# Instance normalisation over 65536 rows: sharing a tile's reductions between ScalarE and VectorE

## The chip, the core and the metric

The kernel runs on one core of one Trainium2 chip. Times are device microseconds of one execution; "span" is the time from the first to the last instruction in a profiled execution, some 2 us less than the execution's own time. ScalarE is ACT in the profile, VectorE is DVE, and SP is the engine whose queue issues every transfer here (SPq and DVEq in the profile are the instruction queues of SP and VectorE). A transfer has landed when its semaphore has its full count; its time to landing runs from its issue to then, so it includes waiting behind earlier transfers.

## The reference

```python
def reference(x, eps):            # x: 256 x 256 x 4096 float32, standard normal
    mean = np.mean(x, axis=2, keepdims=True)
    var = np.var(x, axis=2, keepdims=True)
    return ((x - mean) / np.sqrt(var + eps)).astype(np.float32)
```

So 65536 rows of 4096 numbers, each normalised by itself: 1.07 GB in, as much out, and only a few operations on each number.

## The kernel before

A tile is 128 partitions x 4 rows x 4096 numbers, 8.389 MB, and there are 128 tiles. Three buffers `X[0..2]` hold a tile each; a tile is normalised in place and stored from the same buffer. The first and the last tile are done in two halves of two rows. Semaphores order everything by hand.

SP's loop issues the store of tile t as soon as it is normalised, and right after it the load of tile t+2 into the buffer of tile t-1, whose store was issued a period earlier:

```python
def store(s, t):
    take(S, done[s], K)                      # all K=4 rows normalised
    S.dma_start(out=rows_of(out_t, t), in_=X[s][:, :, :]).then_inc(stored[s], 16)

def load(s, t, wait=True):
    if wait:
        take(S, stored[s], 16)               # the buffer's last store has landed
    S.dma_start(out=X[s][:, :, :], in_=rows_of(x_t, t)).then_inc(loaded[s], 16)
...
with S.Fori(0, rounds) as i:
    for t in range(L0, L0 + BUFS):
        store(t % BUFS, ...)
        load((t + 2) % BUFS, ...)
```

VectorE takes the means of all four rows, one after the other; ScalarE follows a row behind with the sum of squares around the mean (its output goes to a scrap tile in PSUM, and only the accumulated sum is used). Then VectorE normalises rows 0, 1 and 3, ScalarE row 2:

```python
def vector_tile(s, r0=0, k=K, ld=None, dn=None):
    ...
    if ld:
        take(V, ld, 16)
    for r in range(r0, r0 + k):
        ...
        mine(V.tensor_reduce(out=part[s][:, r, :], in_=row, axis=AX.X, op=ALU.add))
        V.wait_ge(own_v, own)
        mine(V.tensor_reduce(out=nsum[s][:, c], in_=part[s][:, r, :], axis=AX.X, op=ALU.add, negate=True))
        V.wait_ge(own_v, own)
        V.tensor_scalar_mul(out=nmean[s][:, c], in0=nsum[s][:, c], scalar1=1.0 / d).then_inc(means, 1)
    last = r0 + k - 1
    for i, c in enumerate((slice(r0, last), slice(last, last + 1))):
        ...                                  # wait for std; rstd and nbias
        for r in range(r0, last - 1) if i == 0 else (last,):
            c = slice(r, r + 1)
            V.tensor_scalar(out=x[:, r, :], in0=x[:, r, :], scalar1=rstd[s][:, c], scalar2=nbias[s][:, c],
                            op0=ALU.mult, op1=ALU.add).then_inc(dn, 1)

def scalar_tile(s, r0=0, k=K, ld=None, dn=None):
    ...
    for r in range(r0, r0 + k):
        ...                                  # wait for the row's mean
        A.activation(out=junk, in_=x[:, r, :], func=AF.Square, bias=nmean[s][:, c], scale=1.0,
                     accum_out=ss[s][:, c]).then_inc(own_a, 1)
    ...                                      # Sqrt; wait for `scaled`
    A.activation(out=x[:, last - 1, :], in_=x[:, last - 1, :], func=AF.Identity,
                 bias=nbias[s][:, c], scale=rstd[s][:, c]).then_inc(dn, 1)
```

## Time and profile before

| | before |
|---|---|
| median of 3 executions | 4965.49 us (4963.85 to 4969.12) |
| span of the profiled execution | 4960.3 us |
| VectorE busy | 3390.1 us (68%) |
| ScalarE busy | 2505.6 us (51%) |
| bytes moved | 2147.52 MB, mean 433 GB/s |

The costliest groups of instructions of the kernel before, from its page: line, engine, operation, what it writes and reads, sizes, count, then the busy time in all and the mean of one in ns, then the engine's idle time before them and what ended most of it.

```profile
L89 DVE TENSOR_REDUCE part<-x 128x64 f32<-128x4096 f32 x512 | 2258.6, 4411 | 1452.4 <-DMA x<-in_x_dram 1452.4
L132 ACT ACTIVATE junk<-x,nmean 128x4096 f32<-128x4096 f32 x512 | 1883.0, 3678 | 2417.0 <-DVE nmean L93 2417.0
L110 DVE TENSOR_SCALAR x<-x,rstd,nbias 128x4096 f32<-128x4096 f32 x382 | 910.2, 2411 | 37.6 <-DVE nbias L102 16.4
L140 ACT ACTIVATE x<-x,nbias,rstd 128x4096 f32<-128x4096 f32 x130 | 492.2, 3786 | 0.0
```

The first line is the dearest work of the kernel, a mean at 4.41 us, and the engine that does it is idle for 1452 us, all of it waiting for loads. ScalarE waits 2417 us for means. These two columns invite the change: ScalarE is idle for want of means, so let it make one.

### The profile page before, as it was taken

How to read it: one execution, taken by the hardware profiler on the slowest of the kernel's cores; microseconds unless marked ns; L12 is line 12 of the kernel's file. 1: busy time of each engine (PE TensorE's matmuls, PEld its weight loads, DVE VectorE, ACT ScalarE, POOL GpSimd, SP SyncE). 2: the span in 40 equal slices, each digit the busy share in tenths (PEclk: the TensorE clock that was granted, in tenths of full speed). 3: DMA queues.
4: the chain of work that ended last, by engine and by line, in shares of the span. 5: the costliest groups of instructions: out<-in, count | busy, mean ns of one | idle time of the engine just before them, and what ended most of it. 6: DMA issues, size and time to landing. Idle time of an engine off the chain costs nothing.

```text
span 4960.3 us, 6348 instructions
## 1 busy us (share of the span) xinstructions
DVE 3390.1 (68%) x2439; ACT 2505.6 (51%) x1416; POOL 0.2 (0%) x4
## 2 busy tenths in 40 slices
DVE  6766666776677766777667776677666776677766
ACT  5555544555445544555445554455544555455545
POOL 0000000000000000000000000000000000000000
DMA  9999999999999999999999999999999999999999
GB/s 423 431 435 430 431 434 433 433 436 433 433 436 432 434 436 432 435 435 433 437 432 434 436 432 434 436 432 433 437 432 434 435 433 435 435 432 438 432 433 406
DMA packets 37299, 2147.52 MB, mean 433 GB/s; under 512 B 4144, under 2 KB 4144, under 8 KB 4144
## 3 DMA queue, kind: packets, MB, share of 16 engines
q1 hardware_dynamic: 37296, 2147.50, 100.0%
q14 instruction: 3, 0.02, 0.0%
HBM read 1073.74 MB, written 1073.74 MB: 433 GB/s over the span
## 4 chain that ended last, share of the span: by engine, by line
DMA 71%; DVE 19%; ACT 7%; another core or an unknown queue 1%; issue 1%; SPq 0%; ACTq 0%; DVEq 0%
DMA x<-in_x_dram 40%; DMA out_dram<-x 31%; DVE part L89 17%; ACT junk L132 3%; ACT x L140 3%; DVE nsum L91 1%; DVE x L110 1%; DVE nmean L93 1%; ACTq L182 0%; ACT std L137 0%; DVE nbias L102 0%; SPq L159 0%; SPq L154 0%; DVE rstd L100 0%
## 5 line engine op out<-in xcount | busy, mean ns | idle before, releaser
L89 DVE TENSOR_REDUCE part<-x 128x64 f32<-128x4096 f32 x512 | 2258.6, 4411 | 1452.4 <-DMA x<-in_x_dram 1452.4
L132 ACT ACTIVATE junk<-x,nmean 128x4096 f32<-128x4096 f32 x512 | 1883.0, 3678 | 2417.0 <-DVE nmean L93 2417.0
L110 DVE TENSOR_SCALAR x<-x,rstd,nbias 128x4096 f32<-128x4096 f32 x382 | 910.2, 2411 | 37.6 <-DVE nbias L102 16.4
L140 ACT ACTIVATE x<-x,nbias,rstd 128x4096 f32<-128x4096 f32 x130 | 492.2, 3786 | 0.0
L91 DVE TENSOR_REDUCE nsum<-part 128x1 f32<-128x64 f32 x512 | 112.4, 220 | 17.7
L132 ACT ACTIVATION_READ_ACCUMULATOR junk<-x,nmean 128x1 f32 x512 | 95.5, 186 | 0.0
L93 DVE TENSOR_SCALAR nmean<-nsum 128x1 f32<-128x1 f32 x512 | 78.5, 153 | 17.5
L100 DVE RECIPROCAL rstd<-std 128x1 f32<-128x1 f32 (+1 forms) x260 | 41.7, 160 | 17.2 <-ACT std L137 16.5
L102 DVE TENSOR_TENSOR nbias<-nmean,rstd 128x1 f32<-128x1 f32 (+1 forms) x260 | 41.6, 160 | 8.9
L137 ACT ACTIVATE std<-ss,eps_tile 128x1 f32<-128x1 f32 x130 | 38.3, 295 | 15.1
L124 ACT ACTIVATE std<-ss,eps_tile 128x3 f32<-128x3 f32 (+1 forms) x130 | 38.5, 296 | 4.2
L132 ACT ACT_TABLE_LOAD x1 | 1.3, 1283 | 1.2 <-DVE eps_tile L211 1.2
L124 ACT ACT_TABLE_LOAD x1 | 1.3, 1283 | 0.0
L211 DVE MEMSET eps_tile<- 128x1 f32 x1 | 0.1, 59 | 1.0 <-SPq L181 1.0
L248 POOL MEMSET const-uint8-127<- 128x1 uint8 x1 | 0.1, 102 | 0.0
L248 POOL MEMSET const-bfloat16-1.0<- 128x1 bf16 x1 | 0.1, 101 | 0.0
L248 POOL MEMSET const-float32-0.0<- 128x1 f32 x1 | 0.1, 98 | 0.2 <-issue 0.2
L248 POOL MEMSET const-float32-1.0<- 128x1 f32 x1 | 0.1, 98 | 0.0
## 6 DMA issues: line engine op xcount, KB each, us to landing
out_dram<-x SPq DMA_DIRECT2D x4, 4096.0 KB, 18.8
x<-in_x_dram SPq DMA_DIRECT2D x2, 4096.0 KB, 16.7
x<-in_x_dram SPq DMA_DIRECT2D x127, 49.2
out_dram<-x SPq DMA_DIRECT2D x126, 30.5
```

The costliest lines, as they stand in the source:

```text
L89: mine(V.tensor_reduce(out=part[s][:, r, :], in_=row, axis=AX.X, op=ALU.add))
L91: mine(V.tensor_reduce(out=nsum[s][:, c], in_=part[s][:, r, :], axis=AX.X, op=ALU.add, negate=True))
L93: V.tensor_scalar_mul(out=nmean[s][:, c], in0=nsum[s][:, c], scalar1=1.0 / d).then_inc(means, 1)
L100: mine(V.reciprocal(out=rstd[s][:, c], in_=std[s][:, c]))
L102: mine(V.tensor_mul(out=nbias[s][:, c], in0=nmean[s][:, c], in1=rstd[s][:, c]))
L110: V.tensor_scalar(out=x[:, r, :], in0=x[:, r, :], scalar1=rstd[s][:, c], scalar2=nbias[s][:, c], op0=ALU.mult, op1=ALU.add,).then_inc(dn, 1)
L124: A.activation(out=std[s][:, r0:last], in_=ss[s][:, r0:last], func=AF.Sqrt, bias=eps_tile, scale=1.0 / d).then_inc(stds, 1)
L132: A.activation(out=junk, in_=x[:, r, :], func=AF.Square, bias=nmean[s][:, c], scale=1.0, accum_out=ss[s][:, c]).then_inc(own_a, 1)
L137: A.activation(out=std[s][:, c], in_=ss[s][:, c], func=AF.Sqrt, bias=eps_tile, scale=1.0 / d).then_inc(stds, 1)
L140: A.activation(out=x[:, last - 1, :], in_=x[:, last - 1, :], func=AF.Identity, bias=nbias[s][:, c], scale=rstd[s][:, c]).then_inc(dn, 1)
L211: V.memset(eps_tile, eps).then_inc(ready, 1)
L248: nc = _bacc.Bacc("TRN2", target_bir_lowering=False, num_devices=1)
```

## The change

The intent is to balance the engines and to shorten a tile. ScalarE takes the mean of row 0 with a Copy that accumulates, while VectorE takes those of rows 1 to 3. The square roots come in two groups, rows 0 and 1, then 2 and 3, so VectorE normalises rows 0 and 1 while ScalarE still squares. Of the last row, ScalarE normalises the first 3072 columns (Q) and VectorE the rest. A new semaphore, `landed`, passes the arrival of a tile from VectorE to ScalarE.

```diff
--- before.py
+++ after.py
@@ -24,6 +24,7 @@
     K = 4
     BUFS = 3
     C = 64
+    Q = 3072
 
     x_flat = x.flatten_outer_dims()
     out_flat = out.flatten_outer_dims()
@@ -62,6 +63,7 @@
     scaled = nc.alloc_semaphore("scaled")
     done = [nc.alloc_semaphore(f"done{s}") for s in range(BUFS + 1)]
     ready = nc.alloc_semaphore("ready")
+    landed = nc.alloc_semaphore("landed")
 
     def take(engine, sem, count):
         engine.wait_ge(sem, count)
@@ -83,7 +85,8 @@
 
         if ld:
             take(V, ld, 16)
-        for r in range(r0, r0 + k):
+        V.sem_inc(landed, 1)
+        for r in range(r0 + 1, r0 + k):
             c = slice(r, r + 1)
             row = x[:, r, :].rearrange("p (c f) -> p c f", c=C)
             mine(V.tensor_reduce(out=part[s][:, r, :], in_=row, axis=AX.X, op=ALU.add))
@@ -92,23 +95,29 @@
             V.wait_ge(own_v, own)
             V.tensor_scalar_mul(out=nmean[s][:, c], in0=nsum[s][:, c], scalar1=1.0 / d).then_inc(means, 1)
         last = r0 + k - 1
-        for i, c in enumerate((slice(r0, last), slice(last, last + 1))):
-            if i == 0:
-                V.wait_ge(stds, 1)
+        groups = [(r0, last - 1), (last - 1, last + 1)]
+        if k == 2:
+            groups = groups[1:]
+        for i, (b, e) in enumerate(groups):
+            c = slice(b, e)
+            final = e == last + 1
+            if final:
+                take(V, stds, i + 1)
             else:
-                take(V, stds, 2)
+                V.wait_ge(stds, i + 1)
             mine(V.reciprocal(out=rstd[s][:, c], in_=std[s][:, c]))
             V.wait_ge(own_v, own)
             mine(V.tensor_mul(out=nbias[s][:, c], in0=nmean[s][:, c], in1=rstd[s][:, c]))
-            if i == 0:
-                V.wait_ge(own_v, own)
+            if final:
+                take(V, own_v, own)
                 V.sem_inc(scaled, 1)
             else:
-                take(V, own_v, own)
-            for r in range(r0, last - 1) if i == 0 else (last,):
+                V.wait_ge(own_v, own)
+            for r in range(b, e):
                 c = slice(r, r + 1)
+                f = slice(Q, d) if r == last else slice(0, d)
                 V.tensor_scalar(
-                    out=x[:, r, :], in0=x[:, r, :], scalar1=rstd[s][:, c], scalar2=nbias[s][:, c],
+                    out=x[:, r, f], in0=x[:, r, f], scalar1=rstd[s][:, c], scalar2=nbias[s][:, c],
                     op0=ALU.mult, op1=ALU.add,
                 ).then_inc(dn, 1)
 
@@ -117,28 +126,39 @@
         x = X[s]
         dn = done[s] if dn is None else dn
         last = r0 + k - 1
-        for r in range(r0, r0 + k):
+        own = 0
+
+        def mine(instruction):
+            nonlocal own
+            own += 1
+            return instruction.then_inc(own_a, 1)
+
+        take(A, landed, 1)
+        c = slice(r0, r0 + 1)
+        mine(A.activation(out=junk, in_=x[:, r0, :], func=AF.Copy, scale=-1.0 / d, accum_out=nmean[s][:, c]))
+        for r in range(r0, last + 1):
             c = slice(r, r + 1)
+            A.wait_ge(own_a, own)
             if r == last:
-                A.wait_ge(own_a, k - 1)
+                take(A, means, k - 1)
+            elif r > r0:
+                A.wait_ge(means, r - r0)
+            mine(A.activation(
+                out=junk, in_=x[:, r, :], func=AF.Square, bias=nmean[s][:, c], scale=1.0, accum_out=ss[s][:, c]
+            ))
+            if r == last or (r == last - 2):
+                c = slice(r0, last - 1) if r == last - 2 else slice(last - 1, last + 1)
+                if r == last:
+                    take(A, own_a, own)
+                else:
+                    A.wait_ge(own_a, own)
                 A.activation(
-                    out=std[s][:, r0:last], in_=ss[s][:, r0:last], func=AF.Sqrt, bias=eps_tile, scale=1.0 / d
+                    out=std[s][:, c], in_=ss[s][:, c], func=AF.Sqrt, bias=eps_tile, scale=1.0 / d
                 ).then_inc(stds, 1)
-                take(A, means, k)
-            else:
-                if r > r0:
-                    A.wait_ge(own_a, r - r0)
-                A.wait_ge(means, r - r0 + 1)
-            A.activation(
-                out=junk, in_=x[:, r, :], func=AF.Square, bias=nmean[s][:, c], scale=1.0, accum_out=ss[s][:, c]
-            ).then_inc(own_a, 1)
-        take(A, own_a, k)
         c = slice(last, last + 1)
-        A.activation(out=std[s][:, c], in_=ss[s][:, c], func=AF.Sqrt, bias=eps_tile, scale=1.0 / d).then_inc(stds, 1)
-        c = slice(last - 1, last)
         take(A, scaled, 1)
         A.activation(
-            out=x[:, last - 1, :], in_=x[:, last - 1, :], func=AF.Identity, bias=nbias[s][:, c], scale=rstd[s][:, c]
+            out=x[:, last, :Q], in_=x[:, last, :Q], func=AF.Identity, bias=nbias[s][:, c], scale=rstd[s][:, c]
         ).then_inc(dn, 1)
 
     def rows_of(ap, t):
@@ -150,7 +170,7 @@
         return ap[bass.ds(i, 1)].rearrange("o p k d -> p (o k) d")
 
     def store(s, t):
-        take(S, done[s], K)
+        take(S, done[s], K + 1)
         S.dma_start(out=rows_of(out_t, t), in_=X[s][:, :, :]).then_inc(stored[s], 16)
 
     def load(s, t, wait=True):
@@ -166,7 +186,7 @@
 
     def store_half(s, t, h):
         r = half_of(h)
-        take(S, second(done, s, h), half)
+        take(S, second(done, s, h), half + 1)
         S.dma_start(out=out_t[t][:, r, :], in_=X[s][:, r, :]).then_inc(second(stored, s, h), 16)
 
     def halves(tile_fn, s, first):
```

## The prediction

> **What bounds the kernel now.** I read the shares of the page first, then the DMA rows of its forty slices, then the waits of the DMA queue, the issues with their times to landing, and at last the timeline of one tile.
>
> ```profile
> DVE 3390.1 (68%) x2439; ACT 2505.6 (51%) x1416; POOL 0.2 (0%) x4
> ...
> DMA  9999999999999999999999999999999999999999
> GB/s 423 431 435 430 431 434 433 433 436 433 433 436 432 434 436 432 435 435 433 437 432 434 436 432 434 436 432 433 437 432 434 435 433 435 435 432 438 432 433 406
> ```
>
> Neither compute engine is full. The DMA engines are, in every slice. A busy share alone could be latency, so the second row matters more: it is flat at 430 to 438 GB/s from the second slice to the last but one. The bytes are fixed: 1073.74 MB read and as much written, 2147.48 MB.
>
> The chain that ended last gives 71% to DMA, and 31% of the span to stores, in pieces of 39 us. That part is misleading. The waits of the SP engine, which issues every transfer, say what held it:
>
> ```profile
> SPq L68 <- ACT x L140: 4759.8, 130, 38.3
> SPq L68 <- DMA out_dram<-x: 44.9, 3, 29.6
> ```
>
> SP waited for a store to land three times in the whole run (the edges), and 130 times for the normalisation. At first sight this says "compute holds the DMA", and a quicker tile should help. The issues show why it doesn't:
>
> ```profile
> x<-in_x_dram SPq DMA_DIRECT2D x127, 49.2
> out_dram<-x SPq DMA_DIRECT2D x126, 30.5
> ```
>
> A tile is 128 x 4 x 4096 x 4 bytes = 8.389 MB. At 434 GB/s it needs 19.3 us of the engines, but a load lands after 49.2 us. The rest must be queueing, and the timeline lets me check it:
>
> ```profile
> 2009.89 0.34 SPq L154 DMA_DIRECT2D out_dram<-x  x1
> 2010.47 0.35 SPq L159 DMA_DIRECT2D x<-in_x_dram  x1
> 2021.13 4.42 DVE L89 TENSOR_REDUCE part<-x 128x64 f32<-128x4096 f32 x1 [11.49 <-DMA x<-in_x_dram]
> ...
> 2045.86 2.41 DVE L110 TENSOR_SCALAR x<-x,rstd,nbias 128x4096 f32<-128x4096 f32 x1
> 2048.46 0.34 SPq L154 DMA_DIRECT2D out_dram<-x  x1
> ```
>
> When the store is issued at 2009.89, the previous load is still on its way; it lands at about 2021.1, 11.2 us later. If the queue is served in order at 434 GB/s, the store lands 11.2 + 19.3 = 30.5 us after its issue, and the load behind it 19.3 us later, 49.2 us after its own issue. Both are the page's medians to a tenth. So at its emptiest the queue still holds 11.2 us of work. The period, 2048.46 - 2009.89 = 38.57 us here and (2125.81 - 2009.89) / 3 = 38.64 us over three tiles, is two transfers: 16.777 MB / 38.64 us = 434.2 GB/s. DMA throughput sets it.
>
> There is also a closed loop: load issue to landing, 49.3, plus compute, 27.3, plus 0.6 between the store's and the load's issue = 77.2 us = two periods (two loads are outstanding in turn). Compute seems to be in the loop, but queueing fills whatever it leaves.
>
> **What the Trainium skill says.**
> - "DMA: Bandwidth & Descriptors", section "Where 436 GB/s comes from": the ports into SBUF top out at 16 x 256 bits x 850 MHz = 435.2 GB/s. The trace's 434.2 is 99.8% of that. The same section says that transfers between HBM and SBUF are bound at about 358 GB/s; this trace disagrees (433 over the span), so I use the port figure.
> - Same page, "Queues, rings and completion order": each DMA engine consumes the descriptors of one ring in ring order. All transfers here are on one queue, and the sums 30.5 and 49.2 agree.
> - "ScalarE: Activation LUTs", "What ACT_TABLE_LOAD costs": 186 ns + 0.833 ns per element with immediate scale and bias, about 93 ns more for each per-partition operand. For 4096 elements, two operands: 3784 ns; the trace has 3786 for the normalisation. One operand: 3691; the trace has 3678 for the square.
> - Same page, "Table sets: the hidden batching unit": copy is in every set as filler. So the new Copy should add no table load; the trace now has just two loads in the run.
>
> **The change part by part, for a tile of four rows.** Durations are from the groups of the page unless said otherwise.
>
> *VectorE.* It loses one mean: 4411 + 220 + 153 = 4.78 us. It normalises rows 0, 1, 2 and a quarter of row 3: the two-row pair took 4.74, a single row 2.41; a quarter I estimate at 0.65 (2.41 / 4 and a little fixed time). So three means 14.34, two pairs of reciprocal and product 0.65, normalisation 4.74 + 2.36 + 0.65 = 7.75: 22.7 us against 3390 / 128 = 26.5. Over 128 tiles some 2910 us (59%).
>
> *ScalarE.* It gains a Copy with accumulation: estimate 186 + 3412 = 3.60 us by the skill's formula, plus 0.19 for reading the accumulator. It loses a quarter of the normalisation: 372 + 0.833 x 3072 = 2.93 instead of 3.79. So per tile 19.6 (2505.6 / 128) + 3.79 - 0.86 = 22.5, in all some 2880 us (58%).
>
> *The tile's path from landing to store.* Before: 2048.46 - 2021.13 = 27.33 us; four VectorE means in series, then the last row's square, root and normalisation. After, on ScalarE, from landing at 0: Copy from 0.15 to 3.9; squares of rows 0 and 1 at 3.86 us each (3.81 from start to the end of the accumulator read, 0.05 of wait) to 11.6; root to 11.9; squares of rows 2 and 3 to 19.6; root, with VectorE going on 0.43 after its start (as at 27.29 and 27.72 in the first tile), to 20.1; reciprocal and product 0.5; then 2.93 on ScalarE beside 3.0 on VectorE: end at 23.7. With 0.2 to the issue: 23.9 us, 3.4 less. VectorE keeps up: its third mean is out at 14.3, rows 0 and 1 are normalised by 19.5, before the second root.
>
> *What lies on the path that sets the end.* In the steady state, nothing of it. Store and load are issued 3.4 us earlier relative to the landing before, so they find 11.2 + 3.4 = 14.6 us of queue. The store lands after 33.9 us instead of 30.5, the load after 52.6 instead of 49.2. The period stays 38.64 us.
>
> *Edges.* First tile: its two half stores go out at 31.4 and 48.2 us. At the latter, by bytes, the queue has until 2 + 20.97 MB / 434 = 50.3 us to go: just enough, so the earlier issue (I estimate 29 and 45 us) gains 0 to 2 us. One stretch, 40 to 45 us, shows only 210 GB/s, but the windows of 38.7 us around it average 406 (with 2 us of start) and 434, so little was really lost. Last tile: its half stores go out at 4926.3 and 4943.5 us. After load 126's landing at 4881.4, load 127 and stores 125, 126 and 127 remain, four transfers or 77.3 us: 4958.7, against a span of 4960.3. The stretch from 4940 to 4945 shows 288 GB/s, so some of the engines may run dry; issuing the last half some 6 us earlier gains 0 to 2 us. Sum: 0 to 4 us, of which I take 2 to 3.
>
> **The rivals.**
> 1. *Compute is in the loop, and its 3.4 us come out.* The SP waits speak for it. If the loop's latency of 77.2 us lost 3.4, the period would lose 1.7 us, 126 x 1.7 = 214 us or 4.3%: 4750 us. Against it: that period is 456 GB/s, above the 434 flat over 4800 us and the skill's 435; and landing times are exactly the sums of queueing.
> 2. *The new order makes the tile slower*: table loads (2 x 1.28 us a tile if Copy or Square switched sets), or a handoff between the engines that I missed. Even then the queue's 11.2 us are a margin: compute could grow from 27.3 to some 38 us before the period moves. This makes it the same time.
> 3. *The transfers themselves slow down*, since the deeper queue changes how reads and writes meet on the engines, or more SBUF reads at once get in their way. Nothing speaks for it: the rate is alike in stretches where both engines work and where neither does, as far as windows of some us show. The first 800 us run at 433 instead of 434 for no reason that I see; if that spread over the run, it would cost 0.2%, 10 us.
>
> **Range and chances.** 4965.5 less 2.5 gives 4963. Downward, the whole edge gain and the 4 us of the slow first 800 us could go together, and the port ceiling of 435.2 for the whole run (4935 us of transfers plus edges) bounds it near 4950; upward, the runs of before spread to 4969 and rival 3 adds a few us. So 4952 to 4971. Over 2% faster would need rival 1 (under 4866 us, or 441 GB/s): 1%. Over 2% slower needs a fault in rival 3: 1%.
>
> **What would show it.** Right: the GB/s row unchanged at 430 to 438; a period of 38.6 us; landings near 33.9 and 52.6; VectorE's wait for the load about 15 us a tile instead of 11.5, SP still waiting on compute 130 times; VectorE near 2910 and ScalarE near 2880 us busy; two table loads. Wrong: landings unchanged with a shorter period (rival 1), a GB/s row below 430 (rival 3), or tiles of over 38 us from landing to store (rival 2).

## The result

| | before | changed |
|---|---|---|
| median of 6 executions | 4964.76 us (4962.69 to 4969.12) | 4966.56 us (4966.29 to 4966.97) |
| span of the profiled execution | 4960.3 us | 4964.2 us |
| VectorE busy | 3390.1 us | 2883.3 us |
| ScalarE busy | 2505.6 us | 2875.8 us |
| landing to store issue, one tile | 27.3 us | 23.7 us |

The ratio is 1.0003, with a 95% interval of 0.9990 to 1.0015: the same. A ratio here is the mean time of one kernel's fast runs over that of the other's fast runs of the same rounds, so not quite the ratio of the medians quoted.

The shares and the DMA rows of the changed kernel, from its page:

```profile
DVE 2883.3 (58%) x2171; ACT 2875.8 (58%) x1672; POOL 0.2 (0%) x4
...
DMA  9999999999999999999999999999999999999999
GB/s 423 430 434 434 431 437 431 436 434 432 437 433 436 432 433 436 433 436 433 433 436 433 435 434 433 437 432 434 435 434 436 432 434 436 434 436 432 433 436 390
```

VectorE lost 507 us of work, ScalarE gained 370, and the row of GB/s did not notice. The groups of instructions show where the work went:

```profile
L92 DVE TENSOR_REDUCE part<-x 128x64 f32<-128x4096 f32 x382 | 1685.6, 4413 | 1899.3 <-DMA x<-in_x_dram 1899.3
L146 ACT ACTIVATE junk<-x,nmean 128x4096 f32<-128x4096 f32 x512 | 1880.7, 3673 | 23.5
L138 ACT ACTIVATE junk<-x 128x4096 f32<-128x4096 f32 x130 | 466.3, 3587 | 1915.1 <-DVEq L70 1915.1
L119 DVE TENSOR_SCALAR x<-x,rstd,nbias 128x4096 f32<-128x4096 f32 (+1 forms) x512 | 1004.2, 2003 | 34.1 <-DVE nbias L110 29.5
L160 ACT ACTIVATE x<-x,nbias,rstd 128x3072 f32<-128x3072 f32 x130 | 383.2, 2948 | 92.9 <-DVEq L70 92.9
```

There are 130 fewer means on VectorE (382 instead of 512), and 130 Copies on ScalarE at 3.59 us. ScalarE's wait of 2417 us for means is gone. But compare the last column of the first line with before: VectorE's wait for loads grew from 1452 to 1899 us. That is 447 us more waiting for 507 us less work; the rest is mostly a longer wait for square roots (from 17 to 87 us, the reciprocal's line). ScalarE's new first instruction waits 1915 us, for VectorE's queue, which passes on the landing (DVEq L70). The work removed has turned into waiting for the same transfers.

The waits of SP in the changed kernel, and its transfers with their median time to landing:

```profile
SPq L70 <- DVE x L119: 4752.8, 130, 38.6
SPq L70 <- DMA out_dram<-x: 55.7, 4, 33.2
```

```profile
x<-in_x_dram SPq DMA_DIRECT2D x127, 52.8
out_dram<-x SPq DMA_DIRECT2D x126, 34.1
```

A store is issued 3.6 us earlier after its tile's landing, and lands 3.6 us later after its issue: 34.1 instead of 30.5 us. A load takes 52.8 instead of 49.2 us. One tile in the timeline of the changed kernel (start and length in us):

```profile
2004.87 0.34 SPq L174 DMA_DIRECT2D out_dram<-x  x1
2005.45 0.35 SPq L179 DMA_DIRECT2D x<-in_x_dram  x1
2019.72 4.42 DVE L92 TENSOR_REDUCE part<-x 128x64 f32<-128x4096 f32 x1 [15.07 <-DMA x<-in_x_dram]
2019.74 3.59 ACT L138 ACTIVATE junk<-x 128x4096 f32<-128x4096 f32 x1 [15.25 <-DVEq L70]
...
2040.16 3.13 DVE L119 TENSOR_SCALAR x<-x,rstd,nbias 128x4096 f32<-128x4096 f32 x2 [0.19 <-DVE nbias L110]
2040.18 2.95 ACT L160 ACTIVATE x<-x,nbias,rstd 128x3072 f32<-128x3072 f32 x1 [0.71 <-DVEq L70]
2043.44 0.34 SPq L174 DMA_DIRECT2D out_dram<-x  x1
```

Both engines begin at the landing, 0.02 us apart, and both end the last row within 0.2 us of each other. The tile takes 2043.44 - 2019.72 = 23.7 us, where it took 27.3. The wait before it is 15.07 us, where it was 11.49. The sum is 38.8 in both kernels, but for hundredths. So the mechanism is as the prediction has it. What it missed is small: it expected 2.5 us less from the edges, and the changed kernel shows none of it.

### The profile page after: what moved, and what is told of

It is laid out like the page before. It is cut to its first block, busy times and chain, and to the rows that moved or that the text cites. A ratio compares the mean times of both kernels' runs of the same rounds, so it can differ in the third digit from the quotient of the medians.

```text
span 4964.2 us, 6467 instructions
## 1 busy us (share of the span) xinstructions
DVE 2883.3 (58%) x2171; ACT 2875.8 (58%) x1672; POOL 0.2 (0%) x4
## 4 chain that ended last, share of the span: by engine, by line
ACT 41%; another core or an unknown queue 37%; issue 12%; DVE 7%; DMA 1%; DVEq 0%; ACTq 0%; SPq 0%
ACT junk L146 31%; ACT junk L138 10%; DVE x L119 6%; ACT std L155 1%; DMA x<-in_x_dram 1%; DVE nbias L110 1%; DVE rstd L108 0%; DVEq L70 0%; ACTq L70 0%; DVEq L234 0%; ACT L155 0%; ACT L138 0%; DVEq L202 0%; ACT x L160 0%
## 5 line engine op out<-in xcount | busy, mean ns | idle before, releaser
L92 DVE TENSOR_REDUCE part<-x 128x64 f32<-128x4096 f32 x382 | 1685.6, 4413 | 1899.3 <-DMA x<-in_x_dram 1899.3
L146 ACT ACTIVATE junk<-x,nmean 128x4096 f32<-128x4096 f32 x512 | 1880.7, 3673 | 23.5
L138 ACT ACTIVATE junk<-x 128x4096 f32<-128x4096 f32 x130 | 466.3, 3587 | 1915.1 <-DVEq L70 1915.1
L119 DVE TENSOR_SCALAR x<-x,rstd,nbias 128x4096 f32<-128x4096 f32 (+1 forms) x512 | 1004.2, 2003 | 34.1 <-DVE nbias L110 29.5
L160 ACT ACTIVATE x<-x,nbias,rstd 128x3072 f32<-128x3072 f32 x130 | 383.2, 2948 | 92.9 <-DVEq L70 92.9
L94 DVE TENSOR_REDUCE nsum<-part 128x1 f32<-128x64 f32 x382 | 84.1, 220 | 13.2
L108 DVE RECIPROCAL rstd<-std 128x2 f32<-128x2 f32 x256 | 41.1, 161 | 87.1 <-ACT std L155 87.1
L155 ACT ACTIVATE std<-ss,eps_tile 128x2 f32<-128x2 f32 x256 | 75.6, 295 | 19.1
L96 DVE TENSOR_SCALAR nmean<-nsum 128x1 f32<-128x1 f32 x382 | 58.7, 154 | 13.1
L110 DVE TENSOR_TENSOR nbias<-nmean,rstd 128x2 f32<-128x2 f32 x256 | 41.2, 161 | 8.8
L138 ACT ACTIVATION_READ_ACCUMULATOR junk<-x 128x1 f32 x130 | 24.2, 186 | 0.0
## 6 DMA issues: line engine op xcount, KB each, us to landing
x<-in_x_dram SPq DMA_DIRECT2D x127, 52.8
out_dram<-x SPq DMA_DIRECT2D x126, 34.1
```

What stands on the lines that cost most here:

```text
L108: mine(V.reciprocal(out=rstd[s][:, c], in_=std[s][:, c]))
L110: mine(V.tensor_mul(out=nbias[s][:, c], in0=nmean[s][:, c], in1=rstd[s][:, c]))
L119: V.tensor_scalar(out=x[:, r, f], in0=x[:, r, f], scalar1=rstd[s][:, c], scalar2=nbias[s][:, c], op0=ALU.mult, op1=ALU.add,).then_inc(dn, 1)
L138: mine(A.activation(out=junk, in_=x[:, r0, :], func=AF.Copy, scale=-1.0 / d, accum_out=nmean[s][:, c]))
L146: mine(A.activation(out=junk, in_=x[:, r, :], func=AF.Square, bias=nmean[s][:, c], scale=1.0, accum_out=ss[s][:, c]))
L155: A.activation(out=std[s][:, c], in_=ss[s][:, c], func=AF.Sqrt, bias=eps_tile, scale=1.0 / d).then_inc(stds, 1)
```

## The experiments

The kernel before stood at 4963.61 us, at 4964.19, at 4963.63, at 4963.22. Each call ran on another chip (5, 2, 6 and 8 in the record). "Measured" gives the median and the ratio to the kernel before on the same chip.

### No compute at all

```diff
         if ld:
             take(V, ld, 16)
+        for r in range(k):
+            V.sem_inc(dn, 1)
+        return                             # nothing below is built
         for r in range(r0, r0 + k):
...
-                halves(scalar_tile, 0, True)   # and all other calls of scalar_tile
```

> The kernel before with all compute taken out: a store is released as soon as its load has landed, so the output is the input, wrong on purpose. Theory (the DMA engines are full and set the period of 38.64 us): the queue only gets deeper, the time stays, 4955 us (4948 to 4967); a store lands after more than 50 us instead of 30.5. Rival 1 (compute is in the loop that sets the period, (49.3 + 0.6 + 27.3) / 2): with the compute gone the period falls to some 25 us and the time to about 3200 us.

Measured: 4960.46 us, ratio 0.9995 (0.9978 to 1.0011). The comparison with the reference passes although the output is the input: a row of 4096 standard normal numbers has a mean near 0 and a deviation near 1 already, and the tolerance is too wide to tell.

The transfers of this run:

```profile
x<-in_x_dram SPq DMA_DIRECT2D x127, 57.7
out_dram<-x SPq DMA_DIRECT2D x126, 57.4
```

Twenty-seven microseconds of compute for each tile, 5900 us of engine time, are worth 3 us in 4964. This is the floor for this order of transfers, and it leaves no room for a version that beats both kernels by changing compute. Rival 1, at 3200 us, is out.

### How much more compute the queue hides

Extra full-row reductions at the head of each tile, into a scrap tile; in the changed kernel they stand ahead of the signal to ScalarE, so they lengthen the whole tile:

```diff
             take(V, ld, 16)
+            for e in range(2):              # 2 or 3 before; 3 or 4 in the changed kernel
+                row = x[:, r0, :].rearrange("p (c f) -> p c f", c=C)
+                mine(V.tensor_reduce(out=idle_out, in_=row, axis=AX.X, op=ALU.add))
+                V.wait_ge(own_v, own)
```

> The kernel before with two more full-row VectorE reductions at the head of every tile, 2 x 4.45 = 8.9 us on its path (27.1 to 36.0 us). Theory: less than the 11.2 us of queue left when a store is issued, so 4965 us within 5; store landings fall from 30.5 to about 21.6 us, load landings from 49.2 to about 40.3. Rival 1: half of 8.9 us on every period, 126 x 4.45 = 560 us more, 5525 us.

> The kernel before with three more full-row reductions, 13.35 us: the tile's serial path becomes 40.4 us, more than the 38.64 us of its transfers. Theory: now compute sets the period: 126 x 40.4 plus about 130 us of edges, 5220 us (5150 to 5260), and VectorE hardly waits for loads any more. Rival 1: 126 x 6.7 more, 5810 us. If the transfers bound it with room to spare, 4965.

> The changed kernel with the same three reductions ahead of the signal that lets ScalarE begin: path 23.5 + 13.35 = 36.8 us, still under 38.64. Theory: 4966 us within 5, so here the change is worth some 5% against the kernel before with the same load, though it is worth nothing without it. Rival (the change slows the transfers or shortens nothing): as slow as the kernel before with three, 5220.

> The changed kernel with four more reductions, 17.8 us: serial path 41.3 us, over 38.64. Theory: compute sets the period, 126 x 41.3 plus some 130 us of edges, 5335 us (5260 to 5380); with three it was the same as without. Rival (the added work is hidden whatever its size): 4966.

| run | measured | ratio to before (95%) | expected |
|---|---|---|---|
| before, 2 more | 5037.26 us | 1.0143 (1.0126 to 1.0160) | 4965 within 5 |
| before, 3 more | 5299.42 us | 1.0677 (1.0659 to 1.0695) | 5220 (5150 to 5260) |
| changed, 3 more | 5086.20 us | 1.0246 (1.0229 to 1.0263) | 4966 within 5 |
| changed, 4 more | 5370.58 us | 1.0819 (1.0801 to 1.0837) | 5335 (5260 to 5380) |

The direction is right: with three extra reductions the changed kernel is 4% faster than the kernel before (5086 against 5299), though it is not faster without them. But three of the four expectations are missed. Two lie just below the limit that I had put at 38.64 us of compute: the queue hides less than I had said. The third, before with three more, took 39 us longer than its range allows, so there the 40.4 us of compute alone did not set the period either. The transfers of the kernel before with three more reductions show why, and three lines of the timeline with two more give the compute of a tile, from landing to the next store (2054.20 - 2017.88 = 36.3 us):

```profile
x<-in_x_dram SPq DMA_DIRECT2D x127, 40.5
out_dram<-x SPq DMA_DIRECT2D x126, 21.7
```

```profile
2016.01 0.35 SPq L164 DMA_DIRECT2D x<-in_x_dram  x1
2017.88 8.87 DVE L89 TENSOR_REDUCE idle_out<-x 128x64 f32<-128x4096 f32 x2 [2.73 <-DMA x<-in_x_dram]
...
2054.20 0.34 SPq L159 DMA_DIRECT2D out_dram<-x  x1
```

With three more, the load ahead lands within 0.6 us of the next store's issue (0.1 us after it in the median of 70 tiles), so the store has next to nothing ahead of it. It still lands only after 21.7 us, not 19.3, and the load behind it after 40.5. Some 2 us of a landing time are latency and not the moving of bytes, so of the 11.2 us that I counted as queue, some 9 were work for the engines. The prediction's closed loop (load landing L, plus 0.58 us between the two issues, plus compute C, equals two periods) then does set the period. With L at 40.5 us, the median of the two slowest runs, the loop stays under 2 x 38.64 us only up to C = 77.28 - 0.58 - 40.5 = 36.2 us. The sum by itself is no test: a load is issued right after a store, its landing starts the compute and the compute ends in a store, so it comes to two periods in the kernel before as well (49.2 + 0.58 + 27.3 = 77.1), where L is full of queueing. What the runs show is that L stops falling: it stays at 40.5 to 40.9 us while C grows by 5.4. The table has L as the page's median of each run (40.9, 40.5, 40.6, 40.5) and C from landing to store issue (36.3 and 37.3 from the timelines of the runs with two and with three; 4.45 more for one further reduction):

| run | C, us | (L + 0.58 + C) / 2 | measured period |
|---|---|---|---|
| before, 2 more | 36.3 | 38.9 | 39.0 |
| before, 3 more | 40.8 | 40.9 | 41.0 |
| changed, 3 more | 37.3 | 39.2 | 39.3 |
| changed, 4 more | 41.7 | 41.4 | 41.5 |

The measured periods are means over 70 tiles each, from the issues of the stores (means over six tiles lie between 38.8 and 39.7 us with two more). The first three rows fit half the loop. In the last row another limit has taken over, as the lines of the extra reductions show for before with three more and changed with four:

```profile
L89 DVE TENSOR_REDUCE idle_out<-x 128x64 f32<-128x4096 f32 x387 | 1710.5, 4420 | 78.9 <-DMA x<-in_x_dram 69.0
```

```profile
L91 DVE TENSOR_REDUCE idle_out<-x 128x64 f32<-128x4096 f32 x516 | 2280.4, 4419 | 26.1 <-DMA x<-in_x_dram 12.1
```

With three more, VectorE still waits 69 us for loads, some half a microsecond a tile. With four more, it waits 12.1 us in the whole run, and that is the first tile: the tiles' compute follows without a break, and the period of 41.46 us is C less the 0.3 us by which one tile's start overlaps the end of the last. So there are three regimes. While the queue never runs dry, transfers set the period and compute is free. Once it does, the period is half the loop, and each microsecond of compute costs half: one more reduction, 4.45 us, took the period of the kernel before from 39.0 to 41.0 us. When C is over L + 0.58, here 41.1 us, half the loop is less than C, and each microsecond should cost a whole one, as it does in the runs with cut stores below (3.6 us of compute, 3.5 us of period). Rival 1 names the right loop, for the wrong side of C = 36.2 us. The kernel before was 8.9 us away from that limit (36.2 - 27.3), the changed one is 12.5 us away (36.2 - 23.7).

The skill's page "DMA: Bandwidth & Descriptors", section "Anatomy of one DMA — SWDGE (gpsimd) path", gives a fixed cost of about 2.0 us beside the moving of the bytes and puts most of it to the confirmation of the last write. It is for another issuing path. The next runs put it at 2.1 us here (an estimate, as worked out there).

### Fewer bytes to store

Only 1024 columns of one row in four are stored (not the edge tiles' halves), so the output is wrong. What isn't stored costs no transfer; all the compute stays:

```diff
-        S.dma_start(out=rows_of(out_t, t), in_=X[s][:, :, :]).then_inc(stored[s], 16)
+        o = rows_of(out_t, t)
+        S.dma_start(out=o[:, 0, :1024], in_=X[s][:, 0, :1024]).then_inc(stored[s], 16)
```

> The kernel before, but a whole-tile store writes only the first 1024 columns of one row in four (0.52 of 8.39 MB), wrong on purpose; the loads are whole. Transfers then need 8.91 MB / 434 GB/s = 20.5 us a tile. Theory: the tile's serial compute of 27.1 us sets the period: 126 x 27.1 plus some 95 us of edges, 3510 us (3450 to 3560). Rival (the loads alone, not the sum of loads and stores, set the 38.64 us): 4965.

> The changed kernel with the same cut stores. Theory: its serial path of 23.5 us is still above 20.5 us of transfers, so 126 x 23.5 plus some 95 us, 3055 us (3000 to 3120): ratio to the kernel before with cut stores 0.87. Rival (the change never shortened the tile): 3510.

Measured: 3513.46 us before and 3067.61 changed, ratio 0.7078 (0.7066 to 0.7089) and 0.6179 (0.6168 to 0.6189) to the whole kernel before, so 0.873 between the two. Periods are 27.06 and 23.5 us, each 0.2 to 0.3 us less than the tile's 27.3 and 23.7 from landing to store: compute without a break. The change is worth 446 us where transfers leave room, and the tile is as much shorter as worked out. The transfers of the changed kernel with cut stores:

```profile
out_dram<-x SPq DMA_DIRECT2D x126, 512.0 KB, 3.3
...
x<-in_x_dram SPq DMA_DIRECT2D x127, 22.4
```

A store of 0.524 MB with nothing ahead takes 3.3 us, of which 0.524 MB / 434 GB/s = 1.2 us is moving the bytes: by this estimate 2.1 us are fixed. The load behind it takes 22.4 us, 1.9 more than the 1.2 + 19.3 of the bytes. This is the term that the margin lacked.

The third run asks which part of the change carries the gain:

```diff
-        V.sem_inc(landed, 1)
-        for r in range(r0 + 1, r0 + k):
+        for r in range(r0, r0 + k):         # VectorE takes all means again
...
-        take(A, landed, 1)
-        c = slice(r0, r0 + 1)
-        mine(A.activation(out=junk, in_=x[:, r0, :], func=AF.Copy, scale=-1.0 / d, accum_out=nmean[s][:, c]))
```

(with ScalarE's waits for means counted to match)

> The changed kernel with cut stores and the first row's mean given back to VectorE; the new grouping and the split last row stay. Theory: the mean is the whole gain. Four means in series (19.1 us), then rows 0 and 1 normalised until 24.2, then reciprocal, product and the last 3.1 us: 27.8 us, 126 x 27.8 plus 95, 3600 us (3500 to 3650), no quicker than the kernel before with cut stores. Rival (the split of the last row carries the gain): near 3055.

Measured: 3595.81 us, ratio 0.7243 (0.7231 to 0.7256), period 27.70 us. This is 2.3% slower than the kernel before with cut stores. The new groups and the split row without the moved mean lose 0.64 us a tile, since VectorE then normalises rows 0 and 1 between its last mean and the last reciprocal. The moved mean is worth 27.70 - 23.5 = 4.2 us a tile in their company. No run moves the mean alone.

### The edges

The changed kernel with the last tile in one piece; and besides, the third buffer's load issued at once:

```diff
-                store_half(last % BUFS, last, 0)
-                store_half(last % BUFS, last, 1)
+                store(last % BUFS, last)
...
-                halves(vector_tile, last % BUFS, False)     # and scalar_tile alike
+                vector_tile(last % BUFS)
```

```diff
                 load(1, 1, wait=False)
+                load(2, 2, wait=False)
                 store_half(0, 0, 0)
                 store_half(0, 0, 1)
-                load(2, 2, wait=False)
```

> The changed kernel with the last tile done and stored as one instead of in two halves. Theory (the tail is four queued transfers of 19.3 us, however early they are issued): the last store is issued before the queue has drained, so 4966 us within 3. Rival (the halves hide part of the last store): 5 to 10 us longer.

> As the run with the whole last tile, and the load of the third buffer issued at once with the first two, not behind the second half store. A try for a version that beats both. Theory: in both kernels the second tile in steady state lands at 82.4 us where four transfers and 2 us of start would allow 79.3, so 0 to 3 us fewer: 4964 us, same. Rival (the start starves the queue for longer than it seems): 5 us or more fewer.

Measured: 4966.67 us for the whole last tile, 4966.65 with the early load too, ratios 1.0002 (0.9982 to 1.0022) and 1.0001 (0.9981 to 1.0021). Neither edge holds anything. The last whole store was issued 32 us before the end of the span (at 4935.5 of 4967.8), where its own bytes need 19.3, so the queue still had work ahead of it. From the landing of tile 126 to the end it took 79.3 us, with the halves 78.7. The early load gives nothing either, so the start was not short of transfers. Neither is a version that beats the two.

### The same two kernels again

The changed kernel unaltered:

> The changed kernel once more, unaltered, for a tighter ratio and a second trace. Both theories of the change (hidden by the queue) say 0.999 to 1.001. Open is where the 4 us between the two profiled spans come from: in the first pair of traces the period was 38.64 us and at some point became 38.74, after about 65 tiles in the changed kernel and about 109 in the kernel before. If that point belongs to the kernel, it lies near tile 65 again; if it is chance, elsewhere.

Measured: 4966.71 us, ratio 1.0002 (0.9982 to 1.0022). The interval is wide since the kernel before had executions of 5014 and 4995 us. Its other ten lay between 4962.36 and 4964.42 us, and the six of the changed kernel between 4966.35 and 4970.83. So a difference of 3 us, 0.06%, is likely, though the intervals do not settle it.

The traces point at where it lies. From about tile 20 on, the period is 38.64 us, and it steps to 38.74 once. Each transfer raises its semaphore sixteen times, once for each DMA engine that has done its share (the skill's page "DMA: Bandwidth & Descriptors", section "Why a DMA increments its semaphore by 16 and not by 1"; the traces hold sixteen increments for each of the 259 transfers). I took from the traces the distance in us from the first to the last of the sixteen, with transfers counted in order of landing, two to a tile:

```
transfer no.      60    110    140    200    240    250
before           6.7    6.8    6.8    6.8    7.4    7.8
changed          5.2    5.2    6.1    9.2   11.2   11.7
changed, again   5.4    5.4    5.8    8.6   10.5   11.0
early load       8.6    8.8    8.8    9.9   11.9   12.4
no compute       6.0    6.0    6.0    6.0    6.1    6.0
```

In the changed kernel the last of the sixteen falls behind by (11.7 - 6.1) / 55 tiles = 0.10 us a tile from about transfer 125 on, which is just the step from 38.64 to 38.74, and it comes at that place in both traces (and with the whole last tile). With the early load it comes some 25 tiles later. The other fifteen increments keep their distances. In the run without compute one of the sixteen increments also moves through the others, from 2.27 us behind the first at transfer 110 to 5.38 at transfer 250, 0.044 us a tile, but it isn't the last yet when the run ends, and the period stays 38.64 us throughout. In the kernel before the same movement is 0.07 us a tile (2.71 to 7.79 us) and the step comes after tile 109. The reading is that one DMA engine is a little slower than the rest, all through the run, and counts only from where it has used up its lead. The trace doesn't name the engines, so that it is one engine is inferred from the even movement. In the first 20 tiles the sixteen increments of a transfer spread apart, from 0.5 or 0.6 us at transfer 4 to 6.5 at transfer 40 in the kernel before, 5.2 changed and 5.8 without compute. In before with two more reductions, where the queue nearly runs dry in each period, they are only 0.5 us apart at transfer 60.

The kernel before once more, to see whether its step has a fixed place:

> The kernel before, unaltered, against itself, for a second trace. In three traces with the changed tile code and the usual start the period steps from 38.64 to 38.74 us after about 65 tiles, and from there on the sixteen increments of one transfer's semaphore lie 0.1 us further apart with each tile; in the one trace of before it steps after about 109. If the step's place belongs to the kernel, it comes near tile 109 again and the time is 4963.5 us; if it is chance, elsewhere (4962 to 4967).

Measured: 4963.02 us, ratio 0.9996 (0.9983 to 1.0010) against itself. The time is as expected, but the profiled execution was one of 5010 us, with five increments 3.8 to 9.2 us behind the first already at transfer 60, and a period near 39.1 us from then on. It isn't comparable, and it tells nothing of the step. So that the slow engine's pace depends on the compute (0.04 without, 0.07 before, 0.10 changed) rests on one trace each of the first two and on few of the last. The traces are also of different chips (5 without compute, 6 for the changed kernel again and its edge runs; that of the first pair is not on record), so the chip is a rival for the pace that no run tests. Why it would depend on either is open.

## Why the prediction was right

**The bound.** The prediction said that transfers in a queue that never runs dry set the period. Taking all compute away moved the time by 0.05%, and storing a sixteenth of the bytes moved it by 29%. Its measured signs came: 34.1 and 52.8 us to landing (33.9 and 52.6 predicted), 15.07 us of VectorE's wait for a load (about 15), SP waiting 130 times for compute as before, and two table loads. One figure against rival 1 is a slip: a period shorter by 1.7 us would be 16.777 MB / 36.94 us = 454 GB/s, not 456, which leaves the argument as it was.

**The change part by part.** VectorE was put at 2910 us and was 2883; ScalarE at 2880 and was 2876; the Copy at 3.60 us and was 3.59; the tile at 23.9 us and was 23.7. The cut-store runs show the same 3.6 us as time: 27.06 against 23.5 us a period.

**Steady state.** Nothing of the 3.6 us came out; it went into queueing, 3.6 us more for each store and each load. That was the prediction's main step, and it holds.

**The edges, mis-sized.** The sum had 0 to 4 us of gain, 2 to 3 taken. The two landings that frame the steady state say otherwise: the third tile (the first after the start) landed at 82.50 us before and 82.38 changed, a gain of 0.1; from the landing of tile 126 to the end it was 78.8 us before (4960.3 - 4881.48) and 78.7 changed (4964.2 - 4885.48). So both edges are worth nothing, as the edge runs confirm. In the start, one term was also wrong: the half stores were to go out at 29 and 45 us, and went out at 31.55 and 47. One part of it is a table load that the prediction did count, but not placed. Its line before, and its line changed, in the timelines:

```profile
1.18 1.28 ACT L132 ACT_TABLE_LOAD   x1 [1.18 <-DVE eps_tile L211]
```

```profile
13.18 1.28 ACT L138 ACT_TABLE_LOAD   x1 [13.18 <-DVEq L70]
```

There are still two loads of 1.28 us in the run, as predicted. But before, the first ran at 1.18 us, while the first tile was in flight. Changed, it runs at 13.18 us, released by VectorE's word that the tile has landed, so it lies on the first tile's path. The likely reason is that the changed code waits and clears a semaphore ahead of its first activation, and the load comes after that; no run tries it otherwise.

**The size of the margin, wrong.** Rival 2 said that compute "could grow from 27.3 to some 38 us before the period moves". It moves at 36.2 us. The step that failed is the use of the 11.2 us of queue as if all of them could be spent; by estimate, some 2.1 to 2.4 us of them are a transfer's fixed latency (3.3 less 1.2 us for the small store, 21.7 less 19.3 for the whole one), which no other transfer covers once nothing else is queued. It made no difference to this change, which went the other way, and three of my expectations fell by it. The prediction's claim that "queueing fills whatever it leaves" holds below 36.2 us of compute only.

**The last 3 us.** The changed kernel is likely 3 us slower rather than 2.5 faster. From tile 20 to tile 61 it led by 1.4 us: tile 61 landed at 2367.49 us, before at 2368.88. At tile 126 it is 4.00 us behind. Nearly all of the 5.4 us between come from the step, 0.10 us a tile, which it reaches some 45 tiles earlier. The increments show one part of a transfer that lags, but not why. The 433 GB/s of the first 800 us, for which the prediction saw no reason, are something else: the run without compute has them too. From tile 2 to tile 20 a tile took 39.0 us in all three (before, changed, no compute: 702.1, 700.9 and 701.3 us for 18 tiles), which is 5 to 7 us more than at 38.64. So compute isn't the cause; it is the stretch in which the sixteen increments spread apart, and whether that costs the time isn't tested.

## What to carry to other kernels

Compare a transfer's time to landing with its bytes over the rate: where a landing time is the sum of what was queued ahead, an engine that waits for compute before it issues is not a sign that compute is the bound. Compute is free only while the queue holds more than one transfer's fixed latency at its emptiest (here 36.2 us of compute under a period of 38.64), so work out the sum of transfers, half the loop and the compute of one tile, and take the largest. Before balancing engines, take out all compute once: 4960 instead of 4964 us says what any rearrangement can gain.

## What the Trainium skill lacked or had wrong

- "DMA: Bandwidth & Descriptors", section "Where 436 GB/s comes from", says that the HBM side binds transfers between HBM and SBUF at about 358 GB/s. Here, loads and stores mixed in one queue went at 434 GB/s in the steady state, 99.8% of the 435.2 GB/s that the section gives for the ports, and at 433 over the whole run. The same page ties the 358 to both cores of an HBM domain streaming; this program runs on one core, so the sentence lacks that condition.
- The same page's "Anatomy of one DMA — SWDGE (gpsimd) path" measured its fixed cost of about 2.0 us on transfers issued from GpSimd. From SP it was an estimated 2.1 us here (3.3 us for a 0.524 MB store, less 1.2 for the bytes). No page says what follows for a loop of load, compute and store: the fixed cost is no longer covered when the queue runs dry, so the period grew at 36.3 us of compute, under the 38.64 us of the transfers.
- No page says that one of the sixteen increments of transfers from SP can fall behind by 0.04 to 0.10 us in each 16.8 MB moved. The page named above knows of two slower engines, but ties them to transfers issued from GpSimd; all of these were issued from SP.
- "ScalarE: Activation LUTs", section "What ACT_TABLE_LOAD costs", gives 2.66 us for a switch, of which 1.38 is a drain. The traces show 1.28 us and the next activation 0.01 us later (13.18 + 1.28, then 14.47 us), with no drain between; the second load is the same (26.03 + 1.28, then 27.33). Nor does the page say where a load falls beside the semaphore waits: in the changed kernel it came after the first landing and lay on the first tile's path.
